# The first output projections as seven block products, between the queries and the attention, with y and the gates passed through DRAM

## The chip, the cores and the metric

The kernel runs on one core of a Trainium2 chip. The metric is the device time of one execution in microseconds (us), taken as the median of several runs. The profile comes from one further execution, recorded by the hardware profiler.

## The reference

Two layers, each on x of 1024 tokens by 1024 features. One wide input projection of the normalised x feeds three branches: four pooling groups, six blocks of a bidirectional recurrence (RG-LRU), and an attention with six query heads on two key/value heads. Each branch is multiplied by its own gate, the results are put side by side (2048 features), and one output projection leads back to x:

```python
z = jnp.einsum('bld,de->ble', rmsnorm(x, norm_g[l]), w_in[l])
u_pool, g_pool, u_lru, g_lru, q, k, v, g_attn = jnp.split(z, splits, axis=-1)
y_pool = pool_mixer(u_pool, pool_w[l], pool_scale[l]) * jax.nn.silu(g_pool)       # 512 features
y_lru = rg_lru_bidir(u_lru, ...) * jax.nn.silu(g_lru)                             # 768 features
y_attn = block_attention(q, k, v) * jax.nn.silu(g_attn)                           # 768 features
x = x + jnp.einsum('ble,ed->bld', jnp.concatenate([y_pool, y_lru, y_attn], -1), w_out[l])
```

## The kernel before

Everything lies transposed: 128 features on the partitions, the 1024 tokens along the free axis; T1 and T2 are the two halves of the tokens. A matmul in full precision is made of three in a faster format: each operand is split into a high part (a cast, mostly on ScalarE) and a low part (the difference, on VectorE), and `mm3` multiplies high by high, high by low and low by high. `proj` streams one weight chunk of 512 KB (`stream_w`: RAW buffer, then WH and WL) and makes 48 matmuls of 512 columns.

The order of the work is not written out: the program records its operations, and a planner (`Plan`) places them on the engines by modelled costs, buffers and priorities (the place of recording, moved by `ahead`). Each engine's queue, and SP's for DMAs, is then issued in that order; POOL issues the DMAs that accumulate (`accumulate`). Buffers come in groups with fixed counts: F (27 tiles of 1024 columns), RAW (3), M (5 tiles of 512 columns), and groups that take over memory from one another: `hT` (the split normalised x, 16 tiles), `at` and `ap` (attention), `st`. In PSUM, `MM` (3 tiles of two banks) and `PS` (6 banks) share six banks, one group after the other, and `SG` has the other two.

A layer runs in this order: pool groups 0 and 1; the six recurrent blocks, whose products with their gates (`lru_gate_out`) are split at once into yh and yl; pool groups 2 and 3; the first output projections (`out_proj` with part 0: eight outputs from pools 0 and 1 and the six recurrent blocks, plus the old x, to x1 in DRAM), about 285 to 374 us in the first layer; the first attention gate; keys and values; queries; gates 1 to 4; and the attention in steps of one head and 128 queries. The sixth gate projection is recorded behind the scores of the first three steps. Beside the attention, `weight_sums` makes sums of weight blocks in DRAM for the second projections.

The second output projections (part 1: pools 2 and 3 and the six attention heads, plus x1) are computed by `Fast` as a 2 x 2 block product with seven products in place of eight. For each pair of outputs, the inputs' eight blocks are taken as two groups of four, d1 and d2, and the tokens as two halves. The seven products use the blocks B11, B21, B22 and the sums t1 to t4; `head` makes the product with B11 into an `MM` tile, `c11` adds the one with B21, and `run` makes the others into `PS` banks and `SG`. A block is one tile with both parts of 512 columns, and `product` is 12 matmuls of 512 columns. The signs of the sums are carried by y itself (`signed`).

Of the kernel before, what the change touches and what calls it, by code (L numbers as in the profile page):

```python
# [437 lines left out]
def record_kernel(nc, ins, outT):  # L438
# [8 lines left out]
    P.group("J", 1)  # L447
    P.group("Q", 2)
    P.group("SG", 2)
    for l in range(L):  # L450
        P.group(f"MM{l}", 3, after=f"PS{l - 1}" if l else None)
        P.group(f"PS{l}", 6, after=f"MM{l}")
        P.group(f"hT{l}", 16, after=f"st{l - 1}" if l else None)
        P.group(f"at{l}", 4, after=f"hT{l}")
        P.group(f"st{l}", 12, after=f"at{l}")
    P.layer = 0

    class ahead:
        def __init__(self, n):
# [12 lines left out]
        return P.tile("F", [128, cols], dt, name)  # L472

    def MM(name="mm"):
        return P.tile(f"MM{P.layer}", [128, 1024], F32, name)

    def bank(name):
        return P.tile(f"PS{P.layer}", [128, 512], F32, name)

    def SM(name="sm"):  # L480
        return P.tile("SG", [128, 512], F32, name)
# [255 lines left out]
            P.vector.tensor_tensor(out=s[:, t], in0=s[:, t], in1=p, op=ALU.mult)  # L737
        return s

    def lru_gate_out(h, s):  # L740
        P.vector.tensor_tensor(out=h, in0=h, in1=s, op=ALU.mult)
        return split(h, T, "y")


    def pool_group(l, g, hT, ups=None, gps=None):
# [217 lines left out]
                P.vector.tensor_tensor(out=y[:, t], in0=y[:, t], in1=o[:, h * 128:(h + 1) * 128], op=ALU.mult)  # L963


    def out_proj(l, part, y, src, dst, halves, norm=None):
        xn_t = []
        for half in halves:
            t0 = half * HALF if half is not None else 0
            n = Norm(t0, HALF) if norm is not None else None  # L970
            cols = HALF if half is not None else T
            for j in range(NK):
                w = stream_w(wo[l, part, j])
                xr = RAW("xr") if half is None else M("xr")
                P.sync.dma_start(out=xr, in_=src[j][:, t0:t0 + cols])
                if half is None:
                    last = (l, part, j) == (L - 1, 1, NK - 1)
                    mm = MM()
                    parts = TAIL if last else ((0, 512), (512, 1024))
                    for a, b in parts:  # L980
                        for k in range(NK):
                            kk = slice(k * 128, (k + 1) * 128)
                            mm3(mm[:, a:b], w[0][:, kk], w[1][:, kk], y[k][0][:, a:b], y[k][1][:, a:b], k == 0, k == NK - 1)
                    for a, b in parts if last else ((0, T),):
                        P.vector.tensor_tensor(out=xr[:, a:b], in0=xr[:, a:b], in1=mm[:, a:b], op=ALU.add)
                        P.sync.dma_start(out=dst[j][:, a:b], in_=xr[:, a:b])
                else:
                    mm = MM()[:, 0:HALF]
                    proj_half(mm, w, y, half)
                    if half == 0:  # L990
                        xn_t.append(F("xn"))
                    xn = xn_t[j][:, t0:t0 + HALF]
                    P.vector.tensor_tensor(out=xn, in0=xr, in1=mm, op=ALU.add)
                    P.sync.dma_start(out=dst[j][:, t0:t0 + HALF], in_=xn)
                    n.add(xn)
            if n is not None:
                with ahead(-LATE if half == 0 else 0):
                    n.finish(*norm)

# [22 lines left out]
    class Fast:  # L1022
# [172 lines left out]
        def c12(self, j, b, w):  # L1195
            self.product(b, w, "B22", False)
            self.add(j, T2, b, ALU.add)
            self.done(j, T2)


    P.group("Q2", 2)
    for l in range(L):
        P.group(f"ap{l}", 4, after=f"hT{l}")
    hT = alloc_hT(0)
    x0 = [F("x0") for k in range(NK)]
    norms = [Norm(*seg) for seg in SEGS]
# [44 lines left out]
        decay_consts()  # L1251

    for l in range(L):
        P.layer = l
        pw = gate_weights(wp[l])
        yp = []
        if l > 0:
            first = [stream_w(wcm[l, CH_UP]), stream_w(wcm[l, CH_GP])]
            firsts = [MM(), MM()]
            for half in range(2):  # L1260
                for w, ps in zip(first, firsts):
                    proj_half(ps[:, half * HALF:(half + 1) * HALF], w, hT, half)
        prev = pool_group(l, 0, hT, *firsts[0:2])
        cur = pool_group(l, 1, hT, *firsts[2:])
        yp.append(split(pool_out(l, 0, pw, *prev), T, "y"))
        prev = cur

        y = []
        xc = lru_conv(l, 0, proj(l, CH_UL, hT))
        yp.append(split(pool_out(l, 1, pw, *prev), T, "y"))  # L1270
        for j in range(NB):
            if j + 1 < NB:
                nxc = lru_conv(l, j + 1, proj(l, CH_UL + j + 1, hT))
            lru = Lru(l, j, gate_weights(wg[l, j]), *xc)
            lru.gates(0)
            s = silu(proj(l, CH_GL + j, hT))
            lru.gates(1)
            y.append(lru_gate_out(lru.scan(), s))
            xc = nxc
        pw = gate_weights(wp[l])  # L1280
        prev = pool_group(l, 2, hT)
        cur = pool_group(l, 3, hT)
        yp.append(pool_out(l, 2, pw, *prev, True))
        prev = cur
# [12 lines left out]
        fast = None  # L1297
        units = [(g, c) for g in range(NG) for c in range(NT)]
# [3 lines left out]
        def scores(n):  # L1302
# [3 lines left out]
            if h == 0:  # L1306
                us[i] = Unit(l, *units[i], qT[units[i][0]])
            att_scores(us[i], h, kT, "F" if n < 3 else f"ap{l}")
        scores(0)
        ws = Fast.weight_sums(l, 1, us[0].first)  # L1310
        scores(1)
        scores(2)
        sg.append(silu(proj(l, CH_GA + 5, hT, singles()), True))
        for n, (i, h) in enumerate(steps):
            if n:
                scores(n + 2)
# [1 line left out]
            if i > 0:  # L1318
                att_pv(us[i - 1], v, sg, h, True)
                if h == GQ - 1 and us[i - 1].g == 0 and us[i - 1].c == NT - 1:  # L1320
                    fast = Fast(l, 1, yp[2:] + sg[0:2], sg[2:6], f"st{l}", ws)
                    with ahead(-100):
                        for k in range(4):
                            fast.early(k)
                        fast.first(0)
                elif h == GQ - 1 and us[i - 1].g == 1 and us[i - 1].c == 3:
                    with ahead(-100):
                        for k in range(1, 4):
                            fast.first(k)
                elif h == GQ - 1 and us[i - 1].g == 1 and us[i - 1].c == NT - 2:  # L1330
                    with ahead(-20):
                        fast.sums(0, 0, HALF, True)
                        for k in range(1, 4):
                            fast.sums(k, 0, 384, True)
# [17 lines left out]
def hymba_kernel(ctx: ExitStack, tc: tile.TileContext, *aps):  # L1352
# [12 lines left out]
    def make(t):  # L1365
# [7 lines left out]
        for of, key, space in ((side, {"hT": "h", "at": "a", "ap": "a", "st": "s"}.get(g[:2]), {}),  # L1373
                               (banks, {"MM": "m", "PS": "p"}.get(g[:2]), dict(space=bass.MemoryType.PSUM))):
            if key is None:
                continue
# [84 lines left out]
```

## Time and profile before

| | |
|---|---|
| median of 3 runs | 1629.21 us (1627.88 to 1629.31) |
| the profiled execution | 1628.12 us, span 1626.3 us |
| TensorE busy | 1609.0 us (99%), 7878 matmuls |
| VectorE busy | 1108.1 us (68%) |
| ScalarE busy | 789.6 us (49%) |
| POOL busy | 113.8 us (7%) |
| granted TensorE clock, mean | 0.997 |
| DMA | 136.87 MB, 84 GB/s over the span |

The span is the time from the first to the last instruction; the execution has 1.8 us more. The busy time of TensorE has to be read with care: matmuls are pipelined, so neighbours overlap, and the spacing of their starts is the cost of one. In the rows further down an operation stands as out<-in by the names of the tiles, xN is the number of instructions, and what stands behind a bar or in brackets is the idle time before, with the one that ended it.

### The profile page before, as it was taken

The page shows a single profiled execution, that of the slowest core. Times are in us where ns is not written, and L with a number is a line of the kernel's source. Part 1 is how long each engine was busy: PE and PEld are TensorE (multiplying, and loading weights), DVE is VectorE, ACT ScalarE, POOL GpSimd, SP SyncE. Part 2 cuts the span into 40 slices and gives each one's busy share as a digit, 9 for nine tenths or more (in the row PEclk, how much of TensorE's full clock was granted, in tenths as well). Part 3 has the DMA queues.
Part 4 walks back from the last instruction along what each step waited for, and adds up shares of the span by engine and source line. Part 5 has one row for each costly group of instructions (what it writes and reads, how often), then busy time and mean ns, then how long its engine had stood idle before and what let it go on. Part 6 is the DMA issues. An engine that isn't in the chain of part 4 may idle for free.

```text
span 1626.3 us, 20051 instructions
## 1 busy us (share of the span) xinstructions
PE 1609.0 (99%) x7878; PEld 1367.7 (84%) x7878; DVE 1108.1 (68%) x1675; ACT 789.6 (49%) x1262; POOL 113.8 (7%) x130
## 2 busy tenths in 40 slices
PE   8999999999999999999999999999999999999999
PEld 8788888888898889998878888888889987999987
DVE  7659889225564489998875688872255635899874
ACT  5357873012332377775342677721133325777731
POOL 1000000000121120101000000000001212101010
PEclk9999999999999999999999999999999999999999
DMA  6110111335111660107331111114431128402172
GB/s 199 39 59 33 59 39 52 127 129 187 37 39 39 181 105 20 33 5 225 113 105 51 46 57 34 62 43 147 155 128 37 40 58 201 76 17 39 32 220 97
DMA packets 51471, 136.87 MB, mean 84 GB/s; under 512 B 5936, under 2 KB 11056, under 8 KB 51248
## 3 DMA queue, kind: packets, MB, share of 16 engines
q1 hardware_dynamic: 41008, 117.88, 21.4%
q0 software_dynamic: 10368, 17.70, 6.9%
q8 instruction: 62, 1.02, 0.3%
q14 instruction: 33, 0.27, 0.1%
HBM read 109.48 MB, written 35.65 MB: 89 GB/s over the span
## 4 chain that ended last, share of the span: by engine, by line
PE 94%; DVE 2%; ACT 1%; issue 1%; DMA 1%; POOL 1%; SPq 0%; ACTq 0%; POOLq 0%
PE mm L430 62%; PE o L430 8%; PE S L430 8%; PE pt L430 5%; PE c L430 3%; PE a L430 3%; PE b L430 3%; PE d L430 1%; POOL ssq L430 1%; PE qtr L430 1%; DMA raw<-wcm 0%; DVE ra L430 0%; DVE hTl L430 0%; SPq L430 0%; DVE sq L430 0%
## 5 line engine op out<-in xcount | busy, mean ns | idle before, releaser
L430 PE MATMUL mm<-hTh,wh 128*128 128x512 f32 x784 | 309.6, 395 | 0.4 <-ACT U L430 0.4
L430 PE MATMUL mm<-hTl,wh 128*128 128x512 f32 x784 | 308.8, 394 | 0.0
L430 PE MATMUL mm<-hTh,wl 128*128 128x512 f32 x784 | 306.6, 392 | 0.0
L430 ACT CAST wh<-raw 128x1024 fp32r<-128x1024 f32 x56 | 58.8, 1050 | 291.4 <-PE mm L430 289.4
L430 PEld LDWEIGHTS mm<-hTh,wh 128*128 128x128 f32 x784 | 147.1, 188 | 35.6 <-ACT U L430 0.9
L430 PEld LDWEIGHTS mm<-hTh,wl 128*128 128x128 f32 x784 | 147.1, 188 | 34.9
L430 PEld LDWEIGHTS mm<-hTl,wh 128*128 128x128 f32 x784 | 147.3, 188 | 32.7
L430 DVE TENSOR_TENSOR wl<-raw,wh 128x1024 fp32r<-128x1024 f32 x65 | 79.2, 1220 | 95.4 <-ACT wh L430 93.1
L430 PE MATMUL mm<-wq,hTh 128*128 128x384 f32 x512 | 133.6, 341 | 0.0
L430 ACT CAST pTh<-pt 128x1024 fp32r<-128x1024 f32 x94 | 94.9, 1012 | 67.2 <-PE pt L430 67.0
L430 DVE TENSOR_TENSOR pTl<-pt,pTh 128x1024 fp32r<-128x1024 f32 x94 | 114.5, 1220 | 15.7 <-ACT pTh L430 15.2
L430 DVE TENSOR_REDUCE st<-S 128x1 f32<-128x1024 f32 x96 | 116.5, 1217 | 3.5 <-PE S L430 3.1
L430 ACT ACTIVATE p<-S,st 128x1024 f32<-128x1024 f32 x96 | 107.5, 1121 | 3.0 <-DVE st L430 3.0
L430 POOL TENSOR_TENSOR ssq<-ssq,mhalf 128x3 f32<-128x3 f32 (+1 forms) x48 | 43.5, 907 | 909.5 <-DVE ssq L430 909.5
L430 DVE TENSOR_TENSOR xr<-xr,mm 128x1024 f32<-128x1024 f32 x16 | 19.5, 1221 | 122.4 <-PE mm L430 122.4
L430 PE MATMUL mm<-yh,wh 128*128 128x512 f32 x256 | 100.8, 394 | 0.0
L430 PE MATMUL mm<-yh,wl 128*128 128x512 f32 x256 | 100.7, 393 | 0.0
L430 PE MATMUL mm<-yl,wh 128*128 128x512 f32 x256 | 100.5, 393 | 0.0
L430 PE MATMUL pt<-ident,p 128*128 128x128 f32 x752 | 97.5, 273 | 0.0
L430 PEld LDWEIGHTS pt<-ident,p 128*128 128x128 f32 x752 | 87.1, 140 | 11.0 <-ACT p L430 1.0
L430 PEld LDWEIGHTS mm<-wq,hTh 128*128 128x128 f32 x512 | 91.5, 189 | 0.0
L430 PE MATMUL o<-pTl,vh 128*128 128x384 f32 x256 | 90.2, 352 | 0.0
(188 smaller groups left out, 3313.0 us busy)
## 6 DMA issues: line engine op xcount, KB each, us to landing
raw<-wcm SPq DMA_DIRECT2D x52, 512.0 KB, 3.8
raw<-wo SPq DMA_DIRECT2D x16, 512.0 KB, 3.9
x<-xr SPq DMA_DIRECT2D x16, 512.0 KB, 2.7
wf<-w SPq DMA_DIRECT2D x16, 512.0 KB, 4.4
xn<-x SPq DMA_DIRECT2D x16, 512.0 KB, 5.5
raw<-wq SPq DMA_DIRECT2D x16, 384.0 KB, 3.3
w<-wo POOLq DMA_DIRECT2D x24, 256.0 KB, 6.8
xr<-xT SPq DMA_DIRECT2D x8, 512.0 KB, 3.7
```

Of the source, the lines that this page charges most:

```text
L430: getattr(real[op.engine], m)(*[res(x) for x in a], **{n: res(x) for n, x in k.items()})
```

## The change

The first output projections leave `out_proj` (which is gone) for a new class `First`, a variant of `Fast` with the same seven products, run behind gates 1 to 5 and before the attention. y is no longer split in the recurrent branch. Each y is written to DRAM with the signs in it (`put`), the sums t1 to t4 are made there by copies on SP and accumulating DMAs on POOL, and `block` loads each block into an M tile and splits it. The weight sums for part 0 are made in the recurrent branch, behind block 1. Outputs of pool groups 2 and 3 and the six gates are written to DRAM (`keep`) and loaded again (`again`). The sixth gate projection comes before `First`. The banks change hands twice in a layer (`P.banks`), and the sums take hT's memory as group `sa`. The scores of the first three steps are recorded ahead of the last block product.

```diff
+    for i in range(2 * L):
+        P.group(f"MM{i}", 3, after=f"PS{i - 1}" if i else None)
+        P.group(f"PS{i}", 6, after=f"MM{i}")
...
+        P.group(f"sa{l}", 16, after=f"hT{l}")
+        P.group(f"at{l}", 4, after=f"sa{l}")
...
-    def lru_gate_out(h, s):
-        P.vector.tensor_tensor(out=h, in0=h, in1=s, op=ALU.mult)
-        return split(h, T, "y")
+    def lru_gate_out(h, s, signs):
+        for t, sign in zip((T1, T2), signs):
+            P.vector.scalar_tensor_tensor(out=h[:, t], in0=h[:, t], scalar=sign, in1=s[:, t], op0=ALU.mult, op1=ALU.mult)
+        return h
...
-    def out_proj(l, part, y, src, dst, halves, norm=None):
...
+    class First(Fast):
...
+        def put(self, k, y):
+            P.sync.dma_start(out=self.d[k], in_=y)
+            if k < 4:
+                return
+            i = k - 4
+            x, y, a, b = self.d[i], self.d[k], self.t13[i], self.t24[i]
+            for o, t in ((a[:, T1], x[:, T1]), (a[:, T2], y[:, T2]), (b[:, T1], y[:, T2]), (b[:, T2], y[:, T1])):
+                P.sync.dma_start(out=o, in_=t)
+            for o, t in ((a[:, T1], x[:, T2]), (a[:, T2], x[:, T2]), (b[:, T1], a[:, T1]), (b[:, T2], b[:, T1])):
+                accumulate(o, t)
+
+        def block(self, n, i, early=0):
+            self.B[n][i] = block("F" if n[0] == "B" else self.group, n)
+            with ahead(early):
+                a, t = {"B11": (self.d[i], T1), "B21": (self.d[4 + i], T1), "B22": (self.d[4 + i], T2),
+                        "t1": (self.t13[i], T1), "t3": (self.t13[i], T2), "t2": (self.t24[i], T1),
+                        "t4": (self.t24[i], T2)}[n]
+                fill(self.B[n][i], self.load(a[:, t], M))
...
+        def run(self, then):
...
+            for n in ("B11", "B21"):
+                for i in range(4):
+                    self.block(n, i, 100)
+            for n in ("t3", "t1", "t2", "t4"):
+                for i in range(4):
+                    self.block(n, i)
+            self.head(0)
+            for p in pairs[1:]:
+                self.head(p)
+                self.c11(*self.todo.pop(0))
+            self.c11(*self.todo.pop(0))
+            for i in range(4):
+                self.block("B22", i)
+            for p in pairs:
...
+                self.product(c_, w3, "t3", True)
+                V.tensor_tensor(out=x2[:, T2], in0=x2[:, T2], in1=c_, op=ALU.subtract)
+                self.product(b, w1, "t1", True)
+                V.tensor_tensor(out=x2[:, T2], in0=x2[:, T2], in1=b, op=ALU.subtract)
+                self.product(d, w2, "t2", True)
...
+                self.product(c_, wa, "t4", False)
+                self.put_x(j2, T1, x2[:, T1], (c_, ALU.subtract))
+                if last:
+                    P.banks += 1
+                    then()
+                self.product(b, w4, "B22", False)
+                self.put_x(j1, T2, self.half_x(j1, T2), (c, ALU.add), (b, ALU.add))
...
-        yp.append(split(pool_out(l, 0, pw, *prev), T, "y"))
+        part0.put(0, pool_out(l, 0, pw, *prev, True))
...
+            if j == 1:
+                part0.ws = Fast.weight_sums(l, 0, lru.last)
+            part0.put(2 + j, lru_gate_out(lru.scan(), s, (1.0, -1.0) if j < 2 else (-1.0, 1.0)))
...
-        out_proj(l, 0, yp[:2] + y, xs[l], x1, [None])
-        yp.append(pool_out(l, 3, pw, *prev, True))
-        sg = [silu(proj(l, CH_GA, hT))]
+        keep(pool_out(l, 2, pw, *prev, True))
+        keep(pool_out(l, 3, pw, *cur, True))
+        keep(silu(proj(l, CH_GA, hT)))
...
-        for h in range(1, 5):
-            sg.append(silu(proj(l, CH_GA + h, hT)))
+        for h in range(1, 6):
+            keep(silu(proj(l, CH_GA + h, hT), h == 5))
...
-        scores(0)
+        def start():
+            for n in range(3):
+                scores(n)
+        part0.run(start)
         ws = Fast.weight_sums(l, 1, us[0].first)
-        scores(1)
-        scores(2)
-        sg.append(silu(proj(l, CH_GA + 5, hT, singles()), True))
+        sg = [again(d) for d in kept[2:]]
```

## Rows read from the trace of the kernel before

**Rows 1.** The page's first part: busy time, share and instructions of each engine.

```profile
PE 1609.0 (99%) x7878; PEld 1367.7 (84%) x7878; DVE 1108.1 (68%) x1675; ACT 789.6 (49%) x1262; POOL 113.8 (7%) x130
```

**Rows 2.** Waits of TensorE: who for whom, us, times, longest us.

```profile
PE b L430 <- DVE xn L430: 3.3, 1, 3.3
PE S L430 <- DVE pTl L430: 3.3, 2, 1.7
```

**Rows 3.** Stretches: length, busy PE, PEld, DVE, ACT, POOL (instructions), clock, DMA, GB/s.

```profile
260.00:280.00 20.00, 20.00 (x88) 16.24 (x87) 19.33 (x21) 6.37 (x6) 0.00 (x0) 1.00 0.15 53
...
320.00:340.00 20.00, 20.00 (x88) 16.25 (x87) 3.22 (x3) 1.05 (x1) 0.00 (x0) 1.00 0.46 158
...
560.00:580.00 20.00, 18.35 (x102) 15.58 (x101) 14.56 (x23) 14.30 (x23) 7.61 (x10) 1.00 0.92 170
```

**Rows 4.** VectorE in order of time: two residual additions of the first projections.

```profile
318.51 1.22 DVE L430 TENSOR_TENSOR xr<-xr,mm 128x1024 f32<-128x1024 f32 x1 [8.77 <-PE mm L430]
...
329.59 1.22 DVE L430 TENSOR_TENSOR xr<-xr,mm 128x1024 f32<-128x1024 f32 x1 [8.73 <-PE mm L430]
```

**Rows 5.** Groups of instructions by form, busy us, mean ns: first projections.

```profile
L430 PE MATMUL mm<-yh,wh 128*128 128x512 f32 x256 | 100.8, 394 | 0.0
```

**Rows 6.** Chain of waits, start us, us: the second projections of layer 1.

```profile
1546.91 19.47 PE a L430 x84
...
1569.35 2.80 PE d L430 x12
...
1600.13 22.27 PE b L430 x96
```

**Rows 7.** Groups by form again: splits, updates and the attention's steps.

```profile
L430 DVE TENSOR_REDUCE st<-S 128x1 f32<-128x1024 f32 x96 | 116.5, 1217 | 3.5 <-PE S L430 3.1
L430 ACT ACTIVATE p<-S,st 128x1024 f32<-128x1024 f32 x96 | 107.5, 1121 | 3.0 <-DVE st L430 3.0
...
L430 ACT CAST pTh<-pt 128x1024 fp32r<-128x1024 f32 x94 | 94.9, 1012 | 67.2 <-PE pt L430 67.0
...
L430 DVE TENSOR_TENSOR wf<-wf 128x512 fp32r<-128x512 f32 x48 | 33.1, 691 | 8.5 <-ACT wf L430 8.2
...
L430 ACT CAST wf<-wf 128x512 fp32r<-128x512 f32 x45 | 28.0, 621 | 109.9 <-PE c L430 34.7 <-PE mm L430 18.3 <-PE b L430 16.5
...
L430 DVE TENSOR_TENSOR t<-sg,t 128x512 fp32r<-128x512 f32 x24 | 15.6, 682 | 0.0
...
L430 DVE TENSOR_TENSOR yl<-gate,yh 128x1024 fp32r<-128x1024 f32 x12 | 14.7, 1225 | 0.0
```

**Rows 8.** Two stretches of the second projections in layer 0, columns as rows 3.

```profile
745.00:765.00 20.00, 20.00 (x88) 16.20 (x87) 18.41 (x39) 12.20 (x22) 2.62 (x3) 1.00 0.87 251
765.00:770.00 5.00, 5.00 (x23) 4.04 (x22) 4.03 (x9) 1.88 (x3) 0.00 (x0) 1.00 1.01 390
```

**Rows 9.** DMA issues: queue, count, size each, median us to landing.

```profile
xn<-x SPq DMA_DIRECT2D x16, 512.0 KB, 5.5
...
w<-wo SPq DMA_DIRECT2D x16, 256.0 KB, 9.7
w<-w POOLq DMA_DIRECT2D x16, 256.0 KB, 5.5
...
t1f<-sg SPq DMA_DIRECT2D x8, 256.0 KB, 2.3
```

**Rows 10.** TensorE in order of time where the attention of layer 0 starts.

```profile
551.39 0.40 PE L430 MATMUL S<-kTh,qh 128*128 128x512 f32 x1
...
566.88 1.03 PE L430 MATMUL pt<-ident,p 128*128 128x128 f32 x8
...
572.71 0.47 PE L430 MATMUL S<-kTh,qh 128*128 128x512 f32 x1 [1.65 <-DVE pTl L430]
...
576.37 0.42 PE L430 MATMUL o<-pTh,vh 128*128 128x384 f32 x1
```

**Rows 11.** A stretch of 2 us behind the longest wait, columns as rows 3.

```profile
820.00:822.00 2.00, 2.00 (x6) 1.51 (x6) 1.64 (x3) 1.43 (x3) 0.00 (x0) 0.50 0.49 182
```

More of the change, by code (lines that the diff above doesn't have):

```diff
@@ L449, in record_kernel @@
     P.group("SG", 2)
+    for i in range(2 * L):
+        P.group(f"MM{i}", 3, after=f"PS{i - 1}" if i else None)
+        P.group(f"PS{i}", 6, after=f"MM{i}")
     for l in range(L):
-        P.group(f"MM{l}", 3, after=f"PS{l - 1}" if l else None)
-        P.group(f"PS{l}", 6, after=f"MM{l}")
         P.group(f"hT{l}", 16, after=f"st{l - 1}" if l else None)
-        P.group(f"at{l}", 4, after=f"hT{l}")
+        P.group(f"sa{l}", 16, after=f"hT{l}")
+        P.group(f"at{l}", 4, after=f"sa{l}")
         P.group(f"st{l}", 12, after=f"at{l}")
-    P.layer = 0
+    P.banks = 0
     class ahead:
@@ L474, in MM @@
     def MM(name="mm"):
-        return P.tile(f"MM{P.layer}", [128, 1024], F32, name)
+        return P.tile(f"MM{P.banks}", [128, 1024], F32, name)
     def bank(name):
-        return P.tile(f"PS{P.layer}", [128, 512], F32, name)
+        return P.tile(f"PS{P.banks}", [128, 512], F32, name)
     def SM(name="sm"):
@@ L963, in att_pv @@
                 P.vector.tensor_tensor(out=y[:, t], in0=y[:, t], in1=o[:, h * 128:(h + 1) * 128], op=ALU.mult)
-    def out_proj(l, part, y, src, dst, halves, norm=None):
[L967 to L998, printed above, removed]
     def block(group, name):
@@ L1201, in record_kernel @@
     P.group("Q2", 2)
     for l in range(L):
-        P.group(f"ap{l}", 4, after=f"hT{l}")
+        P.group(f"ap{l}", 4, after=f"sa{l}")
     hT = alloc_hT(0)
@@ L1253, in record_kernel @@
     for l in range(L):
-        P.layer = l
+        P.banks = 2 * l
         pw = gate_weights(wp[l])
-        yp = []
         if l > 0:
@@ L1262, in record_kernel @@
                     proj_half(ps[:, half * HALF:(half + 1) * HALF], w, hT, half)
+        part0 = First(l, xs[l], x1)
         prev = pool_group(l, 0, hT, *firsts[0:2])
         cur = pool_group(l, 1, hT, *firsts[2:])
-        yp.append(split(pool_out(l, 0, pw, *prev), T, "y"))
+        part0.put(0, pool_out(l, 0, pw, *prev, True))
         prev = cur
-        y = []
         xc = lru_conv(l, 0, proj(l, CH_UL, hT))
-        yp.append(split(pool_out(l, 1, pw, *prev), T, "y"))
+        part0.put(1, pool_out(l, 1, pw, *prev, True))
         for j in range(NB):
@@ L1277, in record_kernel, with keep, again @@
             lru.gates(1)
-            y.append(lru_gate_out(lru.scan(), s))
+            if j == 1:
+                part0.ws = Fast.weight_sums(l, 0, lru.last)
+            part0.put(2 + j, lru_gate_out(lru.scan(), s, (1.0, -1.0) if j < 2 else (-1.0, 1.0)))
             xc = nxc
+        def keep(y):
+            d = P.tile("dram", [128, T], F32, f"kept{l}_{len(kept)}")
+            kept.append(d)
+            P.sync.dma_start(out=d, in_=y)
+        def again(d):
+            y = F("yk")
+            P.sync.dma_start(out=y, in_=d)
+            return y
+        kept = []
         pw = gate_weights(wp[l])
@@ L1320, in record_kernel @@
                 if h == GQ - 1 and us[i - 1].g == 0 and us[i - 1].c == NT - 1:
-                    fast = Fast(l, 1, yp[2:] + sg[0:2], sg[2:6], f"st{l}", ws)
+                    fast = Fast(l, 1, [again(d) for d in kept[:2]] + sg[0:2], sg[2:6], f"st{l}", ws)
                     with ahead(-100):
```

38 lines of the change are left out of this document (35 added, 3 removed).

## Prediction

> **What bounds the kernel now.** I read the page's sum first: TensorE is busy for 99% of the span, VectorE for 68%, ScalarE for 49% [rows 1]. A busy TensorE alone proves little, because matmuls overlap: one with 512 columns shows 394 ns [rows 5], while the next starts after about 231 (below). So the second view is what TensorE waited for: over the whole span no pair of waiter and releaser has more than 3.3 us, and the longest single wait, 3.3 us, lies at the change of layers [rows 2]. Third come the stretches of 20 us: late in the recurrent branch VectorE is at 19.33 of 20 us with TensorE at 20.00, and in the first output projections VectorE has 3.22 us to do while TensorE still shows 20.00 [rows 3]. TensorE's stream sets the end nearly everywhere; a matmul that is taken out is worth its spacing, if the work that replaces it keeps out of TensorE's way.
>
> **The change, part by part.**
> *Matmuls.* One layer's first output projections are 8 outputs x 2 halves x 8 blocks x 3 = 384 matmuls of 512 columns (768 in all; one of the three forms is in rows 5). Two successive residual additions stand 329.59 - 318.51 = 11.08 us apart, which is 48 matmuls, or 0.2308 us each [rows 4]; a layer has 384 x 0.2308 = 88.6 us. The seven products are 4 pairs x 7 x 4 blocks x 3 = 336 matmuls. Their price is in the trace, since the second projections already run so: 84 in 19.47 us, 12 in 2.80, 96 in 22.27, or 0.2318, 0.2333 and 0.2320 each [rows 6]. With 96 at 0.2318 (the heads) and 240 at 0.2333 it is 22.3 + 56.0 = 78.3 us. Gain: 10.4 us a layer with the fractions kept, 20.8 in both.
>
> *The y splits in the recurrent branch go*: 8 per layer, each a ScalarE cast and a VectorE difference of 1.225 us [rows 7]. Two half-size products replace one whole one in `lru_gate_out` and `pool_out`, at some 0.2 us more each. VectorE is eased by some 8 us a layer, but TensorE didn't wait there [rows 2, 3], so I count nothing.
>
> *VectorE and ScalarE in the new stage.* Per layer 28 activation blocks and 28 weight blocks are split: a difference of 0.682 or 0.691 us on VectorE, a cast of 0.621 on ScalarE (some go to VectorE). Per pair seven half-width updates and one whole one are added; I take them at the 0.682 and 1.225 of the differences of their sizes [rows 7]. VectorE: 56 x 0.69 + 4 x 6.0 = 62.6 us in a stage of 78.3, 80%. The tight part is the head, 96 matmuls or 22.3 us. 16 of the block splits fall into it, since they use hT's memory and that comes free only behind the last attention gate projection: 16 x 0.682 + 8 x 0.691 + 4 x 0.682 = 19.2 us, 86% of it. The same part of the second projections has VectorE at 18.41 of 20 us, and TensorE at 20.00 [rows 8]. So the head hides it: 0, and if it doesn't, the stage waits for VectorE by the difference.
>
> *DMA.* Blocks now come from DRAM. In the head that is at most 11 block loads (five wait ahead in the M buffers), two weights, four residual halves and four stores, about 6 MB in 22.3 us or 270 GB/s, against the 390 GB/s that one stretch moved [rows 8]. A load of 256 KB lands after 2.3 us, one of 512 KB in the busy stage after 5.5 [rows 9]. SP issues in order: a store of y waits for VectorE's product, and the weight streams queue behind it, but three RAW buffers hold some 30 us of weights ahead of TensorE. 0, with the second rival as the other end.
>
> *POOL.* `weight_sums` for the first projections (20 accumulating DMAs) and those of the y sums (16) lie in the recurrent branch now, where POOL has nothing else; the key and query norms that POOL computes are queued behind them, and VectorE's scaling of keys and queries waits for these. With landings of 5.5 us [rows 9] in a chain of two, behind a store and a copy, the last sums end some 20 us behind the sixth block's scan, before the first key norm. 0. Beside a VectorE that is busy for 14.56 of 20 us ten such issues took 7.61 us on POOL, 0.76 each [rows 3]. The Trainium skill, page "SBUF — State Buffer", section "SBUF: two separate sides", speaks against this move: while VectorE runs a copy in a two-port mode, GpSimd cannot write the descriptors of its DMAs and the transfer seems blocked. By that rule the accumulates would be drawn out in the branch where VectorE is fullest; these rows show no such block, and I leave it as one of two ways into the third rival.
>
> *Gates and late pool outputs through DRAM* (`keep`, `again`): 8 stores and 8 loads of 512 KB a layer; the first gate is wanted only with the first finished unit, some 20 us into the attention. 0.
>
> *The pause that goes.* Between the pools and keys/values lay 88 us in which VectorE was nearly idle [rows 3]. Afterwards only the first gate projection (11.1 us) lies there, and beside it VectorE has to do two pool outputs, two tables, four key/value weights and a gate weight, some nine whole operations of up to 1.225 us, 11 us in all. Just enough. Nothing can be gained, since TensorE doesn't wait here now; from above I put 3 us a layer, two or three of these operations and their load. I take 0.5.
>
> *The seam to the attention.* Before, the last gate projection lay between the first scores and their transposes: the scores start at 551.39, the transposes at 566.88, and the first product with the values at 576.37, with one wait of 1.65 [rows 10]. Afterwards the cover is only the last block product (2.8 us). I followed it by the durations of the rows (maximum 1.217, exponential 1.121, cast 1.012, difference 1.225 [rows 7]): TensorE has 13.5 us of scores, transposes and rest of that product; VectorE's chain to the first product with the values is 14 to 17 us. So the wait is 1 to 3.5 us in place of 1.65. Bounds are -1 and +6: behind the wait of 3.3 the clock was at 0.50, the 1.2 GHz level [rows 2, 11], which I price at 2 us more; one of 1.65 wasn't. I take +1. The scores also need the PSUM buffers of the block products, and so the subtraction behind the last t4 product; the B22 product behind that covers it: 0 to 1, I take 0.3.
>
> **Sum.** -20.8 + 2 x (0.5 + 1.0 + 0.3) = -17.2 us. The profiled execution took 1628.12 us with a span of 1626.3; that gives 1610.9. The median of the runs, 1629.21, is 1.1 above it, so I forecast a median of **1612**.
>
> **Rivals.**
> 1. *The attention starts bare* (a smaller gain). VectorE still has the last pair's updates while three maxima come at once; the wait passes 3 us and the clock falls, as it did behind the 3.3 us wait [rows 2, 11]. With 6 us at the seam and 3 before keys/values per layer it is -20.8 + 18 + 0.6 = -2.2, **1627**; with half of that, which I hold likelier, 1618. For it: the cover shrinks from 11 us to 2.8. Against it: half of the chain is ScalarE's, which is idle there.
> 2. *The blocks come too late* (slower). The 16 blocks and the residual halves behind them pass five M buffers in the order of recording: 14 loads or 2.8 rounds of landing + 1.6 us (issue, cast, difference), and the PSUM banks of the next part open only when three of the head's additions are done. At 2.3 us that is 10.9 us, at 5.5 it is 19.9, both inside the 22.3 of the head. At the 9.7 us of the loads among the weight sums [rows 9] it is 31.6, a wait of 9.3 and some 2 for the clock; the gain of 10.4 a layer is gone from a landing of 9.4 us on. At 12 us it is 38.1, 17.8 lost a layer: -20.8 + 35.6 + 3.6 = +18.4, **1648**. Against it: the loads of that length ran beside accumulating DMAs, which this stage hasn't.
> 3. *No change.* The pause was needed: keys/values wait for their weights' loads and splits, or POOL's norms stand behind its accumulates. With 10 us a layer the gain is gone: **1629**. Against it: TensorE waits for none of these now, and VectorE has 8 us a layer less to do ahead of them.
> 4. *A better plan.* The planner lays everything anew; the 3.3 us wait and the slow clock behind it (some 5 us in all) vanish, and seam and pause cost nothing: 1629.2 - 20.8 - 5 = 1603, **1602** with a little at the seam.
>
> **How the numbers follow.** Forecast (1603 to 1618) 0.63; first rival 0.18 (1618 to 1626); second 0.10; third 0.05; fourth 0.04. The range 1603 to 1626 leaves out 0.19. About 0.2%, 3.3 us, is what a measurement of this kernel can tell from no change: faster 0.85, same 0.06 (the third rival and the edges of its neighbours), slower 0.09.
>
> **What the profile will show.** Right: 672 matmuls of seven products in place of 768, at 0.232 us; the stage at some 78 us a layer without a wait over 1 us; VectorE at about 80% in it; a wait of 1 to 3.5 us at the attention's start. Wrong: TensorE waiting in the head for a split that waits for an M load; for VectorE at the first subtractions of the block products; for key/value weights some 300 us into the span; a clock below 1 around the attention's start.

## The result and the profile after

The changed kernel takes **1620.56 us** (median of 5 runs, 1615.38 to 1623.30) against 1629.31 us of the kernel before beside it: a ratio of 0.9942, 95% interval 0.9922 to 0.9961. It gained 8.75 us where 17.2 were forecast: faster, by half the amount. That lies inside the whole range (1603 to 1626) but above the forecast's own part of it (1603 to 1618), in the stretch that the prediction gave to its first rival. The profiled execution was the quickest of the five, 1615.38 us with a span of 1613.6; a second set of runs of the same kernel (e1, below) gave 1622.31, and its profile shows the loss more plainly.

The engines, as the first part of the page after has them:

```profile
PE 1592.0 (99%) x7782; PEld 1349.0 (84%) x7782; DVE 1165.4 (72%) x1816; ACT 823.8 (51%) x1345; POOL 172.6 (11%) x202
```

Against [rows 1] TensorE has 96 matmuls fewer, 48 a layer, as counted (384 - 336). What TensorE waited for, in the view of rows 2 (us in total, times, longest), has a new first line:

```profile
PE mm L430 <- DVE sg L430: 5.4, 6, 1.2
PE b L430 <- DVE xn L430: 3.3, 1, 3.3
...
PE S L430 <- DVE pTl L430: 1.2, 2, 0.6
```

`sg` is a pool's gate: TensorE waits for VectorE's product of the pool's result with it. In the kernel before this pair is not among the waits at all. The wait at the attention's start (`S` for `pTl`) went the other way, from 1.7 each [rows 2] to 0.6. Now the stretches, as in rows 3 (length, PE, PEld, DVE, ACT, POOL, clock, DMA share, GB/s): the recurrent branch while the sums are built, the end of the pools, and the head of the new stage:

```profile
160.00:180.00 20.00, 20.00 (x88) 16.18 (x88) 14.07 (x14) 13.51 (x14) 7.34 (x9) 1.00 1.02 232
...
260.00:280.00 20.00, 20.00 (x88) 16.24 (x87) 18.28 (x19) 7.52 (x8) 2.50 (x3) 1.00 0.87 220
280.00:300.00 20.00, 18.56 (x79) 14.43 (x79) 15.38 (x17) 6.18 (x7) 0.81 (x1) 1.00 0.76 248
480.00:500.00 20.00, 19.56 (x85) 15.53 (x84) 16.53 (x27) 12.30 (x22) 0.00 (x0) 1.00 0.96 327
500.00:520.00 20.00, 19.93 (x86) 15.75 (x85) 12.56 (x20) 5.49 (x9) 0.00 (x0) 1.00 0.92 350
```

The line to stop at is 280 to 300: TensorE is idle for 1.44 us, with VectorE busy for only 15.38 us. So VectorE is not full there either; it waits itself. The DMA share at 260 to 280 is 0.87, where the same stretch of before has 0.15 [rows 3].

**Where the time went.** I cut both traces at the same events of TensorE: the first matmul with a weight from `stream_w` (`wh`; "branch" below: in layer 0 it opens the projection for the gate of pool group 1, in layer 1 the input projection of pool group 0), the first product of keys/values, the first product with the values (`o`), and the branch of the next layer (or the end of the last matmul). Lengths in us, each but the last a difference of two start times:

```
                                    before         after    after - before   forecast
layer 0  branch to keys/values      327.76        243.36       -84.4           -88.1
         keys/values to o           190.06        267.16       +77.1           +79.6
         o to the next layer        249.64        250.75        +1.1              0
layer 1  branch to keys/values      362.92        279.32       -83.6           -88.1
         keys/values to o           190.12        266.74       +76.6           +79.6
         o to the last matmul       243.33        244.13        +0.8              0
```

The forecast of the first line is -88.6 for the projections that leave and +0.5 for the pause; that of the second is 78.3 + 1.0 + 0.3. The second line came out 2.5 to 3.0 us better than forecast. The loss is in the first line: 4 us a layer that did not come off between the branch's start and keys/values (in e1's profile 6.9 and 5.7).

### The profile page after: what moved, and what is told of

It is laid out like the page before. It is cut to its first block, busy times and chain, and to the rows that moved or that the text cites. A ratio compares the mean times of both kernels' runs of the same rounds, so it can differ in the third digit from the quotient of the medians.

```text
span 1613.6 us, 20656 instructions
## 1 busy us (share of the span) xinstructions
PE 1592.0 (99%) x7782; PEld 1349.0 (84%) x7782; DVE 1165.4 (72%) x1816; ACT 823.8 (51%) x1345; POOL 172.6 (11%) x202
## 4 chain that ended last, share of the span: by engine, by line
PE 92%; DVE 4%; ACT 2%; DMA 2%; issue 1%; POOL 0%; SPq 0%; ACTq 0%; POOLq 0%
PE mm L430 52%; PE o L430 8%; PE S L430 8%; PE c L430 6%; PE b L430 5%; PE pt L430 5%; PE a L430 4%; PE d L430 3%; DMA raw<-wkv 1%; PE qtr L430 1%; DMA xr<-xT 0%; DVE sg L430 0%; DVE pTl L430 0%; DVE hTl L430 0%; DVE x L430 0%
## 5 line engine op out<-in xcount | busy, mean ns | idle before, releaser
L430 ACT CAST wf<-wf 128x512 fp32r<-128x512 f32 x87 | 53.8, 621 | 191.1 <-PE c L430 57.0
L430 ACT CAST wh<-raw 128x1024 fp32r<-128x1024 f32 x46 | 48.3, 1050 | 144.7 <-PE mm L430 142.7
L430 DVE TENSOR_TENSOR wl<-raw,wh 128x1024 fp32r<-128x1024 f32 x49 | 59.3, 1218 | 72.9 <-ACT wh L430 70.8
L430 PE MATMUL c<-t,wf 128*128 128x512 f32 x384 | 93.8, 395 | 0.1
L430 PE MATMUL a<-B,wf 128*128 128x512 f32 x384 | 90.6, 395 | 0.9 <-ACT p L430 0.9
L430 PE MATMUL o<-pTh,vh 128*128 128x384 f32 x256 | 90.4, 353 | 0.4 <-DVE pTl L430 0.4
L430 PEld LDWEIGHTS a<-B,wf 128*128 128x128 f32 x384 | 72.0, 188 | 18.1 <-ACT p L430 1.7
```

Of the source, the lines that this page charges most:

```text
L430: getattr(real[op.engine], m)(*[res(x) for x in a], **{n: res(x) for n, x in k.items()})
```

## What could take the time: the theories

Three places of the trace offered themselves. **Theory A:** the head of the new stage lives from hand to mouth, because the residual halves stand behind block loads in the M buffers. VectorE in order of time, in the profile after (start, duration, operation, and in brackets the idle time before it with its releaser):

```profile
497.85 0.69 DVE L430 TENSOR_TENSOR wf<-wf 128x512 fp32r<-128x512 f32 x1
501.71 0.69 DVE L430 TENSOR_TENSOR xr<-xr,a 128x512 f32<-128x512 f32 x1 [3.17 <-DMA xr<-xT]
```

VectorE waits 3.17 us for a residual, and the addition frees the bank that TensorE needs at 502.45. **Theory B:** the pools' outputs are now two half-size products, for the signs, and both halves share one PSUM tile with the second half's matmuls. TensorE in the profile after:

```profile
70.83 0.50 PE L430 MATMUL mm<-pml,gwh 128*128 128x512 f32 x1 [0.84 <-DVE sg L430]
...
287.63 0.50 PE L430 MATMUL mm<-pmh,gwl 128*128 128x512 f32 x1 [1.16 <-DVE sg L430]
```

The first half product (0.74 us) is placed as soon as it can be, and a matmul of the other half that is planned behind it waits for it: the fifth of six at 70.83, the sixth at 287.63. In the kernel before, the outputs of groups 0 and 1 were one whole product behind all six matmuls; those of groups 2 and 3 were two halves already, and the plan had both behind all six (group 2: the first half at 287.57, the sixth matmul at 284.75). **Theory C:** at the pools' end, VectorE's queue has the differences of the key/value weights among the last pool sums. A weight that lands late holds the sums behind it, and these hold the pool's matmuls. **C'** adds that the loads land late because of the accumulating DMAs. In e1's profile, the unchanged kernel run again, VectorE and ScalarE show this most plainly:

```profile
282.63 1.05 ACT L430 CAST wkv<-raw 128x1024 fp32r<-128x1024 f32 x1 [5.04 <-DMA raw<-wkv]
283.71 1.23 DVE L430 TENSOR_TENSOR wkv<-raw,wkv 128x1024 fp32r<-128x1024 f32 x1 [3.29 <-ACT wkv L430]
284.86 1.23 DVE L430 TENSOR_TENSOR ws<-ws 128x1033 f32<-128x1033 f32 x1
```

Read it backwards: the pool sum `ws` at 284.86 had nothing to wait for but its place in the queue, the difference ahead of it waited 3.29 us for the cast, and the cast 5.04 us for the load. What TensorE made of it, and the clock behind it (e1, TensorE; then stretches of 2 us, columns as above):

```profile
290.69 0.79 PE L430 MATMUL mm<-pmh,gwl 128*128 128x512 f32 x1 [3.59 <-DVE sg L430]
291.28 0.63 PE L430 MATMUL mm<-hTh,wh 128*128 128x512 f32 x1
```

```profile
288.00:290.00 2.00, 0.00 (x0) 0.00 (x0) 2.00 (x5) 0.48 (x1) 0.00 (x0) 1.00 0.96 217
290.00:292.00 2.00, 1.31 (x3) 1.12 (x4) 2.00 (x3) 0.00 (x0) 0.00 (x0) 0.56 0.76 244
292.00:294.00 2.00, 2.00 (x7) 1.53 (x7) 1.56 (x2) 1.05 (x1) 0.00 (x0) 0.59 0.32 125
```

A wait of 3.59 us, and behind it a granted clock of 0.56 and 0.59 with one matmul of 0.63 us in place of 0.40. The profile of after had 1.16 us at the same place and no lower clock.

## The experiments

The runs came in three groups: e1 to e4; then e2 again and e5 to e7; then e8, e9, and e5 and e7 again. The kernel before had medians of 1630.5, 1629.87 and 1629.39 us beside them. The length "branch to keys/values" is the first line of each layer in the table above, from the profile of each. Every edit makes the planner lay out the whole program anew, so the lengths tell more than the medians.

**e1, the changed kernel again.** No edit.

> The changed kernel unchanged, to see where its executions differ (1615.4 to 1623.3 us so far, with mean clocks from 0.998 to 0.996). Theory A (residual halves behind the block loads, just in time in the profiled execution): an execution of 1620 us or more shows a wait of TensorE of 3 us or more in front of the first c products of the new stage, with a clock of 0.5 behind it; one of 1615 shows under 0.5 us there. Rival: the difference lies at the change of layers or in the recurrent branch, and the new stage is the same in both.

Measured: 1622.31 us (1620.69 to 1623.82), ratio 0.9951 [0.9939, 0.9963]; branch to keys/values 246.6 and 280.5. Head of the stage and seam are the same in both profiles to 0.3 us, while TensorE's total wait for `sg` is 9.0 us against 5.4. Theory A's wait of 3 us in front of the first c products is 0.33 here. What differs between these two executions lies at the pools' end, not in the head.

**e2, half products behind all six matmuls** (theory B alone).

```diff
-            mm3(ps[:, sl], ...)
+            end = mm3(ps[:, sl], ...)
...
-            P.vector.scalar_tensor_tensor(out=s[:, t], in0=ps[:, t], ...)
+            P.follow(P.vector.scalar_tensor_tensor(out=s[:, t], in0=ps[:, t], ...), end)
```

> The two half products of each pool output are recorded to follow the last of its six matmuls, as the one whole product did before. Theory B (the second half's matmuls wait for the first half's product, since the two share a tile; eight places, 5.4 us of waits of TensorE in the trace): 5 to 7 us faster than the changed kernel, and no wait of mm for sg in the trace. Rival: the wait only moves (to the split of the next pool or to the key/value weights), under 2 us faster.

Measured: 1620.78 us (1617.99 to 1622.81), 0.994 [0.9927, 0.9953]; branch to keys/values 244.0 and 281.1. The waits of 0.84 us are gone (TensorE is full from 60 to 100 us), and still nothing was gained that stands out from the spread: the wait moved. TensorE in e2, layers 0 and 1:

```profile
290.16 0.70 PE L430 MATMUL mm<-pmh,gwh 128*128 128x512 f32 x2 [3.10 <-DVE sg L430]
```

```profile
1090.35 1.19 PE L430 MATMUL mm<-pmh,gwh 128*128 128x512 f32 x2 [3.98 <-DVE sg L430]
```

TensorE came to the pools' end earlier and waited there longer (7.1 us in both layers, 5.6 in e1, 2.0 in the profile of after), until the same late weight. Once more, in the second group:

> The kernel with the pool halves behind the last matmul, once more beside the next three on the same chip: 1619 to 1622 us, and a wait of TensorE of 3 to 4 us (with a slow clock behind it) where the pools end.

Measured: 1619.92 us (1617.08 to 1625.08), 0.9950 [0.9936, 0.9963]; branch to keys/values 242.9 and 279.7, with waits of 3.5 and 2.4 us. The clock fell behind the second of them only.

**e3, residual halves of the head in hT's memory** (theory A alone).

```diff
-            self.put_x(2 * p, T1, self.half_x(2 * p, T1), (a, ALU.add))
+            self.put_x(2 * p, T1, self.half_x(2 * p, T1, F), (a, ALU.add))
```

> The four residual halves of the head get F tiles, so that they no longer queue behind the 16 block loads for the five M tiles. Theory A (the PSUM banks of the block products open only after these halves, and their order behind the blocks makes that late): 3 to 6 us faster than the changed kernel in the median, a spread under 3 us, and the three additions to a done before the last a product ends. Rival: DMA bandwidth in the head (some 400 GB/s) is the limit whatever the order: within 2 us of the changed kernel, the wait then at a split of a t block.

Measured: 1618.61 us (1615.97 to 1621.00), 0.9926 [0.9912, 0.9940]. The residuals now come early, and TensorE's wait for `xr` in the stage (0.3 us in e1, none in the profile of after) is gone; the stage takes 77.4 and 77.2 us in place of 77.9 and 77.3. The median is 3.7 us below e1's beside it, as theory A had asked, but the spread is 5 us and the stage gave only 0.1 to 0.5 us. Theory A's mechanism is there at that size; the rest of the 3.7 lies elsewhere (e9 below comes back to it).

**e4, e2 and e3 together.**

> Both edits together. If both theories hold the gains add: 8 to 13 us faster than the changed kernel, 1607 to 1613 us. If only the pool outputs matter: 1614 to 1616; if neither, 1619 to 1621.

Measured: 1617.81 us (1613.90 to 1621.97), 0.9925 [0.9910, 0.9940]; a wait of 4.0 us at the pools' end remains. That lies between the second and the third expectation, so the gains don't add.

**e5, e2 and the key/value weights behind the pools' sums** (theory C). The casts of the four weights are made to follow the last split of pool group 3, so none of their differences stands ahead of a pool sum in VectorE's queue.

```diff
-        split_to(h, lw, raw)
+        cast = split_to(h, lw, raw)
+        if name == "wkv":
+            P.follow(cast, P.pools)
...
         cur = pool_group(l, 3, hT)
+        P.pools = P.low
```

> As that kernel, and the splits of the key/value weights follow the last split of the pools, so that VectorE no longer stands before a late weight load with the pool sums queued behind it. Theory C (this head-of-line wait costs TensorE 3 to 4 us and the clock behind it some 2 a layer, and is what differs from run to run): 7 to 11 us faster than the kernel beside it, 1609 to 1613 us, spread under 3 us, no wait over 1 us at the pools' end. Rival (VectorE simply has too much to do there): the wait moves to the first key/value matmuls, under 3 us faster.

Measured: **1610.20 us** (1609.02 to 1611.42), 0.9880 [0.9866, 0.9893], 9.7 below e2 beside it.

> The kernel with both edits of the recurrent branch (pool halves behind all six matmuls, key/value splits behind the pools' sums) once more, beside the other three: 1610 us again, with the lower clock behind the layer change's wait of 3.3 us.

Measured: 1609.76 us (1606.72 to 1613.36), 0.9878 [0.9862, 0.9893].

In e5, TensorE's waits no longer have the pair with `sg`; the longest is again that of before:

```profile
PE b L430 <- DVE xn L430: 3.3, 1, 3.3
PE mm L430 <- ACT hTh L430: 1.5, 1, 1.5
```

Branch to keys/values is 239.1 and 275.5. The kernel before without its 88.7 us of projections (384 matmuls of 0.231) has 239.1 and 274.2. And the loads did not come sooner. The DMA issues of the weights near 280 us (count, size, median us to landing), first in e1, then in e5:

```profile
raw<-wkv SPq DMA_DIRECT2D x4, 512.0 KB, 7.7
```

```profile
raw<-wkv SPq DMA_DIRECT2D x4, 512.0 KB, 6.2
```

6.2 us is longer than in the profile of after (5.2), and TensorE doesn't wait. It is the order on VectorE that turns the landing into a wait.

**e6, less traffic** (theory C'). Leaves out part of the computation: the four copies and four accumulating DMAs a layer that make the sums with the eighth y; the blocks that need them load the plain y.

```diff
-            if k < 4:
+            if k < 4 or k == 7:
                 return
...
+                if i == 3 and n[0] == "t":
+                    a = self.d[7]
```

> The changed kernel without the copies and accumulating DMAs for the last y (the sixth recurrent block's; the four sums of that quarter are left out and plain y is loaded in their place). Order on VectorE at the pools is the same. Theory C' (the weights are late because these transfers fill the DMA engines just then): the loads of the key/value weights land in 4 to 5 us in place of 5 to 8, VectorE's wait there falls under 1 us, 3 to 7 us faster than the changed kernel (1615 to 1618). Rival (the loads are late for want of RAW buffers or by SP's order): no faster than 1620.

Measured: 1617.15 us (1615.31 to 1619.09), 0.9922 [0.9909, 0.9934]; branch to keys/values 243.0 and 279.2. The weights land after 3.6 us (before: 3.4), and the longest wait for `sg` is 0.8:

```profile
raw<-wkv SPq DMA_DIRECT2D x4, 512.0 KB, 3.6
```

```profile
PE mm L430 <- DVE sg L430: 5.1, 6, 0.8
```

With less of the sums' traffic (164 GB/s at 260 to 280 us, 220 in the profile of after) the loads are not late, and what is left are six waits of 0.84 us, the shared tile of theory B. The planner laid this kernel's branch out anew as well, so that its order has a part in this that I can't take out; e8 keeps the traffic and changes the order alone.

**e8, the order for the key/value weights alone** (e5's edit without e2's).

> The changed kernel with the order for the key/value weights alone; the pool halves share their tile as in the changed kernel, and the residual halves stay in the M buffers. If the two causes add, the pause before keys/values is worth what separated the two kernels with and without this order (1619.9 and 1610.2: 9.7 us) and the shared tile keeps its 0.84 us beside each first half of pools 0 and 1, 3.4 us in both layers: about 1613 us. If the shared tile matters beside the pools' last sums too (eight places, 5.4 us), about 1615 to 1616. If the order helps only together with the other edit, it stays at the changed kernel's 1620 to 1622.

Measured: 1617.55 us (1614.20 to 1618.65), 0.9919 [0.9907, 0.9931]; branch to keys/values 242.5 and 278.6. It meets e6: six waits of 0.8 are left, as there, though the traffic is all there. It lies between the second expectation (1615 to 1616, for four places a layer) and the third (1620 or more, if the edits only help together), some 2 us from either. From e8 to e5 the stretch shrinks by 3.3 and 3.0 us: the price of the shared tile, 6.4 us in both layers, is more than the 5.1 us of its six waits. A wait is counted from the end of the matmul before it, and what it costs is the spacing of the starts: in the profile of after the fourth, fifth and sixth matmul of the first pool start at 69.59, 70.83 and 71.17, which is 1.1 us more than two steps of 0.23, for a wait of 0.84. That the tile is what ties the two halves is read from which matmul waits for which product; no run gave each half a tile of its own. The profiles of the two differ further at the kernel's start (1.3 us) and at the change of layers (1.2), which the last section takes up.

**e7, all three edits, and e9, e8 with the residual halves in hT's memory.**

> All three edits: pool halves, key/value splits behind the pools, and residual halves in F. If the residual halves matter, 2 to 4 us faster than the kernel without that edit, 1606 to 1611; if what they seemed to bring came from the wait at the pools' end, the same within 1 us.

> All three edits once more. If the residual halves are worth some 5 us by themselves: 1605 again. If the lower clock at the layer change made the difference, the profile shows it this time or not, and the median lies within 2 us of the kernel beside it where it does.

> The same with the four residual halves of the head in hT's memory. The last two pairs with and without this edit were 3.7 us (1622.3 to 1618.6) and 5.2 us (1610.2 to 1605.0) apart, with only 0.1 to 0.5 us a layer to be seen in the head. If the edit has an effect of its own: 4 to 5 us below the kernel beside it, about 1609. If those differences were the clock's, which fell behind the layer change's wait in some executions and not in others: less than 2 us below it.

Measured: e7 **1605.02 us** (1603.70 to 1607.17), 0.9849 [0.9836, 0.9863], and again 1606.56 (1603.81 to 1609.36), 0.9853 [0.9840, 0.9867]; this is the fastest kernel of the study, 24.9 and 22.8 us under the kernel before. e9: 1615.32 us (1615.19 to 1618.09), 0.9915 [0.9901, 0.9928]. So the residual halves bring 5.2 and 3.2 us beside e5, and 2.2 beside e8, in medians (3.7 from e1 to e3). In the profiles about 2 us of that come back each time, all in layer 1: branch to keys/values 275.5 and 275.6 (e5), 274.1 and 274.0 (e7), 278.6 (e8), 277.4 (e9); the new stage 77.8 to 78.0 (e5, e8) and 77.3 (e7, e9). TensorE shows 20.00 of 20 us in these stretches of e5 and e7 alike, with 87 to 88 matmuls in the one and 88 in the other: the same stream runs some 0.5% slower without a wait. The traces tell which matmuls: in layer 1's stretch the next matmul starts 232 ns behind a product of `hTh` with `wl` (the high part of x by the low part of a weight) in every profile without this edit (after, e1, e2, e5, e6, e8), and 229 ns behind it in every one with it (e3, e4, e7, e9), in the kernel before, and in layer 0 of all of them. There are 336 such products in a layer, and the other two forms lose up to 0.8 ns each. Why a choice of buffers changes that, no run tells. The rest of the difference is not the edit's: e7 and its repetition, the same program, differ by 5.6 us of span in their profiles, 4.1 ahead of the branch of layer 0 (it starts at 58.08 and 62.19) and 1.6 at the change of layers.

The stretch from the branch to keys/values, in one table:

```
                     layer 0         layer 1       longest wait for sg
before, less 88.7    239.1           274.2         none
after, e1            243.4, 246.6    279.3, 280.5  1.2, 3.6
e2, repeated         244.0, 242.9    281.1, 279.7  4.0, 3.5
e3                   244.9           278.5         2.7
e4                   244.9           277.8         4.0
e6                   243.0           279.2         0.8
e8                   242.5           278.6         0.8
e9                   242.5           277.4         0.8
e5, repeated         239.1, 239.1    275.5, 275.6  none
e7, repeated         239.1, 239.1    274.1, 274.0  none
```

Two causes in a row explain it. Each shared tile costs its wait; and the late weight sets a time ahead of which the last pool sums can't be made. Take the first away alone (e2), and TensorE only arrives sooner at the second: between 2.5 us lost and 4.5 gained, by which profiles one sets side by side. Take the second away alone (e8), and the first remains: 1.6 us gained (from after) to 6.0 (from e1). Both away (e5), and the stretch is what it was before without the projections, but for 1.3 us in layer 1: the slower stream, which goes with the residual halves (e7). What either is worth hangs on the other: with the tile mended, the order is worth 7.9 to 10.5 us (e2 to e5), and with the order mended, the tile is worth 6.4 (e8 to e5).

## Why the prediction was half right

The sign, the matmuls and the new stage were right. The size was not, and that the time still fell into the range is luck: it lies in the part of the first rival, whose mechanism (a bare start of the attention) did not come, and one of the prediction's own signs of being wrong, a wait for the key/value weights some 300 us into the span, did (at 288 to 291 us, by way of the pool sums).

- **Matmuls, -20.8: right.** 96 matmuls fewer. From the stage's first product to the first scores it takes 77.6 us in layer 0, with 329 of its 336 matmuls; the other seven stand behind the scores and take 1.6, together 79.2 where 78.3 were put in. The projections' 88.7 us left without a rest: e7's stretch is 239.1 and 274.0.
- **The new stage, 0: right to a us, with less room for the DMAs than I thought.** VectorE is busy for 55.95 of its 77.6 us, 72% (80% forecast), in the head for 16.53 of 20. The DMA engines carried 327 GB/s in the head and 350 behind it, against the 270 that I had estimated for the head. The second rival's mechanism is in the trace, the residual that VectorE waits 3.17 us for, but it comes just in time: TensorE's wait for it is 0.5 us at most in any profile (e5 repeated), and moving it (e3) took 0.1 to 0.5 us off the stage. Its 2.3 us for a load of 256 KB was not a load from DRAM: `t1f<-sg` copies between two SBUF tiles. The block loads landed as the page after has them, far from the 9.4 us at which the gain would have gone:

```profile
wf<-t SPq DMA_DIRECT2D x32, 256.0 KB, 4.0
...
wf<-yd SPq DMA_DIRECT2D x24, 256.0 KB, 2.9
```

- **The seam, +1 a layer: wrong to the good side.** TensorE's waits there are 0.61 for the scores and 0.21 for the first product with the values, 0.8 in place of 1.65 [rows 10]. I had VectorE's chain at 14 to 17 us against 13.5 of TensorE's work; from the first score to the first such product it took 14.2 us. The lower end of the chain was the right one. No lower clock followed. Without the gate projection of before (11.1 us of 24.98) and the seven block matmuls of after (1.6 of 14.2), the seam took 13.9 us then and 12.6 now, 2.6 a layer better than the +1.3 that I had put in.
- **POOL, 0: right for its queue.** (What the traffic of its DMAs cost stands further down.) The issues of its accumulating DMAs take 0.81 to 0.86 us each in layer 0's branch (one of 36 took 1.03), beside a VectorE that is busy for 14.07 to 19.30 of 20 us from 160 to 200 us. Before, whole issues in the stretch of [rows 3] took 0.82 to 0.85; my 0.76 came of two that the window cuts. The stretch where VectorE is fullest, in the profile after (columns as above; POOL is the fifth of the busy times):

```profile
180.00:200.00 20.00, 20.00 (x88) 16.16 (x87) 19.30 (x18) 14.34 (x17) 6.62 (x9) 1.00 0.92 173
```

  The rule of the Trainium skill, page "SBUF — State Buffer", section "SBUF: two separate sides", is about issues beside a VectorE that copies in a two-port mode. My prediction stretched it to a VectorE that is merely full. This trace is no test of the rule: in these 20 us VectorE runs products, sums and scans, and one cast of 0.43 us at 199.75. A block in another form isn't shown either. Between issues for the weight sums POOL sits idle for 1.7 us in the mean with nothing that the profile shows to release it, but it did so in the kernel before too, beside the attention (116.4 us in 68 places after, 58.9 in 34 before).
- **"The pause that goes", +0.5: this step failed.** Its list of work stands in the trace. What it lacked was the order and the landing. I added up VectorE's operations as if they could be made in any order, and argued from "TensorE doesn't wait here now". But VectorE takes them as queued; the planner, with 88 us less room, put the weights' differences between the pool sums; and the loads that they wait for land in 5 to 8 us and not in 3.4, beside DMAs that I had counted at 0 (without eight of these a layer, in e6, it is 3.6). It measured 0.8 and 3.0 us a layer in the mean where the shared tiles wait too (after and e1 against e8; in e1 with the clock that fell behind the 3.59 us wait), and 3.9 to 5.3 without them (e2 against e5), so that even my upper bound of 3 was short. This is the third rival's mechanism, "keys/values wait for their weights' loads and splits", at half of its 10 us a layer or less, and with the pool sums as the ones that wait.
- **"Two half-size products ... so I count nothing": this step failed too.** I costed VectorE's time, which was indeed free, and not what the product shares with TensorE. Two products on one PSUM tile, the first placed ahead of the last matmuls, make these wait: 3.3 and 3.0 us in the two layers (e8 to e5). For groups 0 and 1 the halves are new; the third wait of each layer, at the pools' end, comes of the new order, since group 2 had its halves before and no wait.
- **Sum.** From the table: two times 88.7 us less, 77.1 and 76.6 more, and 1.9 behind the attention's start make -21.8; without the failed steps the kernel e7 has -22.8 to -24.9. The failed steps took 8.0 us of it in the profile of after and 12.4 in e1 (both against e5), and the slower stream in layer 1 another 1.4, which no term of the sum had; that leaves 12.4 and 8.0, and the medians gained 8.75 and, in e1's group, 8.2. The forecast was off by less than these errors because the seam repaid some 5 us of them. The 1.9 us behind the attention's start had no term either, and no run looked for their cause.

## What to carry to other kernels

When work that gave an engine slack is moved away, don't add up what is left for it; write its queue down in order and look for an operation that waits for a load ahead of one that the bounding engine waits for. A load's landing has to be taken from a stretch with the DMA traffic that the change will put there. When one whole operation becomes two halves, ask which tile both share with the engine that fills it, and let the first half start behind the last write. Try such mends together as well as one by one: here the one alone moved the median by about 1 us (e2), the other by 3 to 5 (e8), both together by 10 to 12 (e5).

## What the runs showed of the hardware

The clock's answer to a wait isn't the same from one execution to the next. The wait of 3.3 us at the change of layers is in every profile here. In e7 and in its repetition, one program, it is followed by these 24 matmuls (TensorE; start, time from the first's start to the last's end):

```profile
807.51 5.80 PE L430 MATMUL b<-B,wf 128*128 128x512 f32 x24 [3.31 <-DVE xn L430]
```

```profile
811.58 7.38 PE L430 MATMUL b<-B,wf 128*128 128x512 f32 x24 [3.31 <-DVE xn L430]
```

In the first the granted clock stayed at 1.00; in the second it is 0.50, the 1.2 GHz level, from 813 to 815:

```profile
813.00:815.00 2.00, 2.00 (x6) 1.53 (x5) 1.44 (x3) 1.44 (x3) 0.00 (x0) 0.50 0.49 191
```

That is 1.6 us for the same wait, and I had priced it at 2. The first profile of e7 is the only one of the 14 in which the clock stayed up there. At the pools' end the length of a wait didn't decide it either: behind waits of 3.50 us (e2 repeated, layer 0) and 3.62 us (e4, layer 1) the clock stayed at 1.00, behind one of 2.37 us (e2 repeated, layer 1) it went to 0.50.

The kernel's start, with short waits in it, moved the begin of layer 0's branch from 57.7 to 62.2 us between profiles; in the latest of them (e7 repeated) the clock is 0.68 from 10 to 20 us and 0.81 from 20 to 30, in the profile of after 0.83 and 1.00. Two kernels that differ by under 5 us in single profiles can therefore not be ranked by their spans; stretches cut at the same events can where no such wait is in them: branch to keys/values repeats to 0.1 us in e5 and in e7, and differs by 3.2 us in layer 0 between after and e1, which have the late weight in it.

Second, the landing of one and the same load: 512 KB of key/value weights took 3.4 and 4.1 us in the kernel before (layers 0 and 1; it loads them later, beside a DMA share of 0.64 at 370 to 390 us), 5.0 to 7.7 in the changed kernel with the accumulating DMAs beside it (after and e1; share 0.87 and 0.83 at 260 to 280 us), and 3.6 and 3.5 with eight of their copies and accumulates a layer left out (e6; share 0.72).
